# Two-pass stacked products of 64 rows and a split pooled product in a two-block network

## The chip, the cores and the metric

The kernel runs on one core of a Trainium2 chip. Its time is the device time of one execution in microseconds (us), given as the median of several runs. The core has a matrix engine (PE), a vector engine (DVE), an activation engine (ACT), a general engine (POOL), a sync engine (SP) that mostly issues DMAs, and DMA engines that move data. Each engine works through its own list of instructions in order.

## The reference, cut to what matters

The program takes 512 tokens of width 1024 through two blocks. The first block has an "even" mixer (multi-scale pooling beside a state-space scan) and an "odd" mixer (gated convolution). The second block has four feed-forward layers and two mixers: `mix0` (differential attention beside an RWKV-7 layer) and `mix1` (native sparse attention, "NSA", beside an mLSTM). All in float32. What the change touches:

```python
# even mixer: four groups of 128 channels
mixed = einsum('bsgc,gcd->bsgd', pooled, pool_w) * pool_scale
# mix0, differential attention: 4 heads, 2 components of 64 each
s = einsum('bhcqd,bhckd->bhcqk', q, k);  p = softmax(where(mask, s, -1e30))
attn = p[:, :, 0] - lam_full * p[:, :, 1]
# mix0, RWKV-7: low-rank gates of rank 64, 64 and 128
w = -softplus(-(w0 + tanh(wl) @ w2)) - 0.5;  a = sigmoid(a0 + al @ a2);  g = sigmoid(gl) @ g2
# mix1, NSA: 8 heads of 64 in 2 groups, three sets of keys
sc = einsum('bghqd,bgnd->bghqn', q, k_cmp)   # 31 compressed blocks
ss = q @ ks;  sw = q @ kw                    # selected (all 8 blocks here) and window keys
```

## The kernel before, in words

Activations lie with channels on the 128 partitions and the 512 tokens along the free side. A "dense" product (`form1`) takes one 128-column slab of weights: SP loads it as float32 (tile `st`, 3 buffers), ACT writes its fp16 high part and DVE the fp16 remainder (`wh`, `wl`), and PE makes, for each 128 rows, three fp16 products (L309 to L311) into one PSUM bank. `split` (L290, L291) divides an activation in the same way: ACT writes the high part, POOL (or DVE) subtracts to get the low part.

The order of the instructions on each engine is made by a scheduler when the program is built. It takes the program's order as priority, and raises the RWKV work of `mix0` over the rest. PSUM banks and SBUF tiles come from pools with fixed buffer counts. A tile that shares a `tag` with another uses the same buffer, so it waits until the other one has been read.

`even` (the trace's 0 to 250 us): the pooled groups multiply `pool_w` by the pooled tile `pd` in one float32 product each (L818).

`mix0` (about 850 to 1212 us): 22 dense products are made in `AB_ORDER`. After the v of each RWKV head pair, `rwkv_prepare` runs for that pair; `rwkv_solve` and `rwkv_chain` follow. `rwkv_prepare` loads `lora` (tile of its own), makes two float32 products of 64 rows by 512 columns (L1022, L1050) with the shared tile `wa`, and later inverts 16 by 16 blocks from the tile `Lb` (L1096, L1098). `rwkv_chain` makes one float32 product of 128 rows with the gate tile `gs` (L1234). Each of four differential heads gets q and k through `rope` (four DMAs that swap halves, L994; two POOL products, L995 and L996; one DVE sum, L997), then for each of four query tiles two float32 score products of 64 rows (L1268), softmax, and the values. At the end `project_out` adds the result to x: first the heads 0 to 2, then the rest, which needs the last head and the last RWKV pair.

`mix1` (about 1910 to 2210 us): the queries of one pair of heads at a time are made, rotated and split into `nq`. `nsa_pair` then makes, for each query tile and each of three key sets, six fp16 products of 64 rows (L1573): high-high, low-high, high-low, each for the two heads of the pair, which lie on rows 0 to 63 and 64 to 127. The keys stand in two copies with the halves exchanged (`ks`, `ksx`). The rope of the next pair's query shares the buffers of the tag `swap` with `nw`, which the pair before still uses.

A float32 product appears as two instructions in the trace.

Of the kernel before, what the change touches and what calls it, by code (L numbers as in the profile page):

```python
# [10 lines left out]
F32 = mybir.dt.float32  # L11
# [14 lines left out]
FS = 16.0  # L26
NEG = -1e30
WINDOWS = (2, 4, 8, 16)
LAM_INIT = 0.8 - 0.6 * math.exp(0.0)
# [156 lines left out]
class Net:  # L186
# [106 lines left out]
    def later(self):  # L293

        if self.due:
            self.due[0] -= 1
            if not self.due[0]:
                _, v, r = self.due
                self.due = None
                self.reciprocal(v, r)  # L300

    def form1(self, src, kn, xh, xl, w=None):
# [462 lines left out]
    def even(self):  # L765
        nc, A = self.nc, self.A
        V, G = nc.vector, nc.gpsimd
        with ExitStack() as c:
# [5 lines left out]
            tp = open_("e_t")  # L774
            pw = self.const(sp, "pool_w", [P, 4, P])
            cnt = self.const(sp, "c_cnt", [P, 4, 16])
            vec = self.const(sp, "ev_vec", [P, 2, 4])
# [18 lines left out]
            yl = self.parts("hl")  # L796

            for g in range(4):
                ps = self.form1(A["ev_in"][4 + g], KD, hh, hl)
# [207 lines left out]
    def rwkv_prepare(self, i, K, sp, tk, wk, r, k, v):  # L1007
# [16 lines left out]
        nc.scalar.activation(ld, ps, AF.Tanh, scale=0.5, bias=K["w0h"][:, i:i + 1])  # L1024
        cd = -0.5 * math.exp(-0.5)
# [22 lines left out]

        ps = self.aux()
        nc.tensor.matmul(ps, lora[64:128], K["wa"][64:128], start=True, stop=True)  # L1050
        a = tt("ta")
        nc.scalar.activation(a, ps, AF.Tanh, scale=0.5, bias=K["a0h"][:, i:i + 1])
        V.tensor_scalar(a, a, 0.5, 0.5, op0=ALU.mult, op1=ALU.add)
# [150 lines left out]
    def rwkv_chain(self, R, K, wk, yh, yl):  # L1204
# [5 lines left out]
        g2 = wk.tile([P, P], F32, name="g2")  # L1210
        nc.scalar.dma_start(g2, self.A["lora"][:, 1, i * P:(i + 1) * P])

        ps = self.aux().rearrange("p (a b) -> p a b", a=8)
# [39 lines left out]
    def diff_head(self, h, K, dk, yh, yl, q, k, vt):  # L1253
# [53 lines left out]
    def mix0(self):  # L1307
        nc, A = self.nc, self.A
        V, G = nc.vector, nc.gpsimd
        with ExitStack() as c:  # L1310
# [41 lines left out]
            V.scalar_tensor_tensor(K["lamf"], le[:, 0:1], LAM_INIT, le[:, 1:2], op0=ALU.add, op1=ALU.subtract)  # L1352
            K["wa"] = sp.tile([P, T], F32, name="wa")
            K["gs"] = sp.tile([P, T], F32, name="gs")
            yh = self.parts("hh")
# [28 lines left out]
            def take(n, ps):  # L1384
                if n < 2:
                    t = tk.tile([P, T], F32, name="ta")
                    shifted(ps, n, t)
                    if n == 0:
                        nc.scalar.activation(K["wa"][0:64], t[0:64], AF.Tanh)
                        V.tensor_copy(K["wa"][64:128], t[64:128])  # L1390
                    else:
                        nc.scalar.activation(K["gs"], t, AF.Tanh, scale=0.5)
                        V.tensor_scalar(K["gs"], K["gs"], 0.5, 0.5, op0=ALU.mult, op1=ALU.add)
                elif n < 14:
# [7 lines left out]
                else:  # L1402
                    h, j = divmod(n - 14, 2)
                    s = tk.tile([P, 1 + T], F32, name="raw", bufs=2)[:, :T]
                    self.scaled(s, ps)
                    d = dk.tile([P, T], F32, name="qr" if j == 0 else "kr", bufs=2)
                    self.rope(dk, d, s, cs)
                    got["qk"[j]] = d
                    if j == 1:
# [133 lines left out]

    def halves(self, pool, name, src, bufs=1, eng=None):

        r = pool.tile([P, 2, T], F16, name=name, bufs=bufs)
        self.split(r[:, 0], r[:, 1], src, eng)
        return r

    def nsa_pair(self, i, K, nk, yh, yl, q):  # L1550
# [6 lines left out]
        st = {}  # L1557
        hs = (slice(0, 64), slice(64, 128))

        def scores(qt, j):  # L1560
            n = (qt + 1) * P
            if j == 0:
                st[qt] = (nk.tile([P, 2, 3], F32, name="nmx", bufs=3), nk.tile([P, 2, 3], F32, name="nls", bufs=3))
                m, mask = 31, K["cmpm"][:, qt]
                keys = lambda hb, c: K["kcmp"][hs[hb], c, g * 31:g * 31 + 31]
            else:
                m, mask = n, K["causal"][:, 384 - qt * P:512]
                keys = lambda hb, c: K[("ks", "kw")[j - 1]][g != hb][hs[hb], c, :n]
# [109 lines left out]
    def mix1(self):  # L1678
        nc, A = self.nc, self.A
        V, G = nc.vector, nc.gpsimd  # L1680
        with ExitStack() as c:
# [34 lines left out]
            def keys(j):  # L1716
# [3 lines left out]
                self.rope(nk, s, s, cs)  # L1720
                d = self.halves(sp, n, s)
                e = sp.tile([P, 2, T], F16, name=n + "x")
                nc.sync.dma_start(e[0:64], d[64:128])
                nc.scalar.dma_start(e[64:128], d[0:64])
                K[n] = (d, e)

# [104 lines left out]
```

## Time and profile before

| | us |
|---|---|
| median of 3 runs (lowest, highest) | 2565.97 (2560.58, 2567.92) |
| profiled execution, its own time | 2559.88 |
| profiled execution, span from first to last instruction | 2558.1 |
| PE busy | 2462.0 (96%) |
| DVE busy | 1397.3 (55%) |
| ACT busy | 940.7 (37%) |
| POOL busy | 734.6 (29%) |

Busy time is the union of an engine's instructions. PE instructions overlap: a matmul's row tells how long one takes from entering to leaving, while the next may start earlier, so what a product costs is read from one start to the next. "Idle before, releaser" names what an engine's wait ended with.

### The profile page before, as it was taken

Reading aid. Unit: us, or ns where it says so; the run is one execution under the profiler, and the core shown is the slowest. Engines: PE = TensorE matmul, PEld = TensorE weight load, DVE = VectorE, ACT = ScalarE, POOL = GpSimd, SP = SyncE. Lnnn points to the kernel's source line nnn. Section 1 sums busy time; section 2 is a strip of 40 time slices with the busy share of each in tenths; the row PEclk is TensorE's granted clock in tenths of the full one; section 3 lists DMA queues with packets and bytes.
Section 4 is the critical chain, followed back from the end, with each engine's and each line's share of the span. In section 5 each row is a group of like instructions: output and inputs, shape, how many; then the busy total and the mean of one; then the engine's idle time right before and its main releaser. Section 6 shows DMA issues by size and latency. Waiting matters only on the chain.

```text
span 2558.1 us, 36794 instructions
## 1 busy us (share of the span) xinstructions
PE 2462.0 (96%) x14453; PEld 1259.9 (49%) x14453; DVE 1397.3 (55%) x2383; ACT 940.7 (37%) x1598; POOL 734.6 (29%) x657
## 2 busy tenths in 40 slices
PE   6998989999999999999999999999999999899998
PEld 3554434444444456674444444444457565444445
DVE  8945897743333767757433334333345777733334
ACT  3223665533322333334323223322232566523322
POOL 4820760333310332322333201333003122333300
PEclk9889999999999999999999999999999999999999
DMA  5314221233333321114333333333335201333334
GB/s 158 88 52 124 83 66 50 85 100 104 99 112 123 108 66 48 45 27 138 100 105 101 97 101 107 100 100 102 99 105 160 65 24 47 95 102 105 97 105 124
DMA packets 108853, 237.66 MB, mean 93 GB/s; under 512 B 38920, under 2 KB 48264, under 8 KB 108680
## 3 DMA queue, kind: packets, MB, share of 16 engines
q1 hardware_dynamic: 93024, 226.93, 29.5%
q10 hardware_dynamic: 15656, 8.39, 1.2%
q8 instruction: 113, 1.85, 0.3%
q14 instruction: 60, 0.49, 0.1%
HBM read 222.69 MB, written 7.34 MB: 90 GB/s over the span
## 4 chain that ended last, share of the span: by engine, by line
PE 82%; DVE 7%; issue 4%; POOL 4%; DMA 2%; ACT 1%; SPq 0%; POOLq 0%; ACTq 0%; DVEq 0%
PE b L310 16%; PE b L309 16%; PE b L311 16%; PE b L513 6%; PE b L512 6%; PE b L511 6%; POOL cv L928 3%; PE b L1155 1%; DVE wl L283 1%; PE b L1573 1%; PE mm L311 1%; PE mm L310 1%; PE b L1593 1%; PE mm L309 1%; PE b L1268 1%
## 5 line engine op out<-in xcount | busy, mean ns | idle before, releaser
L309 PE MATMUL b<-hh,wh 128*128 128x512 f16 x2096 | 795.4, 382 | 22.2 <-ACT hh L290 8.2
L282 ACT ACTIVATE wh<-st 128x1024 f16<-128x1024 f32 (+6 forms) x432 | 422.1, 979 | 1065.1 <-PE b L310 634.0
L310 PE MATMUL b<-hl,wh 128*128 128x512 f16 x2096 | 798.0, 381 | 1.0 <-POOL hl L291 1.0
L311 PE MATMUL b<-hh,wl 128*128 128x512 f16 x2096 | 796.6, 381 | 0.4 <-DVE wl L283 0.4
L283 DVE SCALAR_TENSOR_TENSOR wl<-st,wh 128x1024 f16<-128x1024 f32 (+6 forms) x432 | 512.7, 1188 | 331.1 <-ACT wh L282 330.3
L310 PEld LDWEIGHTS <-wh 128*128 128x128 f16 x2320 | 228.9, 99 | 292.5 <-issue 34.0
L309 PEld LDWEIGHTS <-wh 128*128 128x128 f16 x2320 | 229.4, 99 | 288.4 <-issue 19.7
L311 PEld LDWEIGHTS <-wl 128*128 128x128 f16 x2320 | 228.6, 99 | 284.1 <-issue 19.1
L513 PE MATMUL b<-fh,wl 128*128 128x512 f16 x660 | 250.4, 379 | 0.0
L512 PE MATMUL b<-fl,wh 128*128 128x512 f16 x660 | 250.4, 379 | 0.0
L511 PE MATMUL b<-fh,wh 128*128 128x512 f16 x660 | 250.3, 379 | 0.0
L500 POOL TENSOR_TENSOR sg<-sg,rho 128x512 f32<-128x512 f32 x88 | 153.5, 1746 | 292.8 <-ACT sg L499 282.2
L291 POOL TENSOR_TENSOR fl<-f,fh 128x512 f16<-128x512 f32 x88 | 139.7, 1587 | 265.7 <-ACT fh L290 265.5
L503 DVE SCALAR_TENSOR_TENSOR f<-b,sg 128x512 f32<-128x512 f32 x88 | 60.8, 691 | 246.1 <-PE b L311 240.0
L335 DVE TENSOR_TENSOR sg<-b,rho 128x512 f32<-128x512 f32 x88 | 60.4, 691 | 232.3 <-PE b L311 228.8
L291 POOL TENSOR_TENSOR hl<-nh,hh 128x512 f16<-128x512 f32 x45 | 59.5, 1329 | 298.4 <-ACT hh L290 298.4
L513 PEld LDWEIGHTS <-wl 128*128 128x128 f16 x660 | 64.6, 98 | 77.9
L512 PEld LDWEIGHTS <-wh 128*128 128x128 f16 x660 | 64.6, 98 | 77.9
L511 PEld LDWEIGHTS <-wh 128*128 128x128 f16 x660 | 64.6, 98 | 77.8
L309 PE MATMUL mm<-hh,wh 128*128 128x512 f16 x224 | 87.2, 393 | 10.6 <-ACT hh L290 8.7
L928 POOL TENSOR_TENSOR cv<-cv,cvt 128x512 f32<-128x512 f32 x60 | 88.1, 1470 | 15.2 <-ACT cvt L927 10.8
L310 PE MATMUL mm<-hl,wh 128*128 128x512 f16 x224 | 87.8, 394 | 3.2 <-POOL hl L291 2.0
(605 smaller groups left out, 3032.6 us busy)
## 6 DMA issues: line engine op xcount, KB each, us to landing
st<-in_gu_a SPq DMA_DIRECT2D x88, 512.0 KB, 3.5
st<-in_gu_b SPq DMA_DIRECT2D x88, 512.0 KB, 3.5
st<-in_dn_b SPq DMA_DIRECT2D x36, 512.0 KB, 3.5
st<-in_dn_a SPq DMA_DIRECT2D x32, 512.0 KB, 3.5
st<-in_od_in SPq DMA_DIRECT2D x24, 512.0 KB, 3.5
st<-in_ab_in SPq DMA_DIRECT2D x22, 512.0 KB, 3.6
st<-in_cd_in SPq DMA_DIRECT2D x16, 512.0 KB, 3.7
st<-in_ev_in SPq DMA_DIRECT2D x15, 512.0 KB, 3.7
```

The source lines that it names most:

```text
L282: nc.scalar.activation(wh[:, s], st[:, s], AF.Copy, scale=WS)
L283: nc.vector.scalar_tensor_tensor(wl[:, s], st[:, s], WS, wh[:, s], op0=ALU.mult, op1=ALU.subtract)
L291: (eng or self.nc.gpsimd).tensor_sub(lo, src, hi)
L309: self.nc.tensor.matmul(ps, wh[:, s], xh[:, k], start=(k == 0), stop=False)
L310: self.nc.tensor.matmul(ps, wh[:, s], xl[:, k], start=False, stop=False)
L311: self.nc.tensor.matmul(ps, wl[:, s], xh[:, k], start=False, stop=(k == kn - 1))
L500: nc.gpsimd.tensor_mul(sg, sg, self.rho)
L503: nc.vector.scalar_tensor_tensor(f, ps, 1.0 / FS, sg, op0=ALU.mult, op1=ALU.mult)
L511: nc.tensor.matmul(ps, wh[:, s], fh[:, k], start=(k == 0), stop=False)
L512: nc.tensor.matmul(ps, wh[:, s], fl[:, k], start=False, stop=False)
L513: nc.tensor.matmul(ps, wl[:, s], fh[:, k], start=False, stop=(k == KF - 1))
L928: G.tensor_add(cv, cv, t)
```

## The change

New helpers: `halves` (moved) splits a tile into high and low fp16 parts. `stack` copies these, by four DMAs within SBUF, so that for each 64-row half e the high part lies on its own rows and the low part on the other 64 rows of a 128-row tile. `twice` copies the high part of a 64-row half onto both halves, also by four DMAs. `stacked` makes scores from them: one product of 128 rows per head (high and low query parts against the high key parts, in one pass), and one of 64 rows (high query part against low key parts).

Differential scores, NSA scores and the two RWKV low-rank products of 64 rows use this form; the gate product and the pooled product become three fp16 products. The low-rank weights are loaded twice over (four DMAs a pair) into a tile that shares the tag `Lb`. `rope` of the differential heads now writes in place, and the stacked parts share the tag `swap`; in NSA the parts share the tag `sm`. The softmax tile `pe1` has one buffer instead of two.

```diff
+    def stack(self, dst, src):
+        for e, q in enumerate(HALF):
+            self.nc.sync.dma_start(dst[q, e], src[q, 0])
+            self.nc.sync.dma_start(dst[HALF[1 - e], e], src[q, 1])
+    def twice(self, dst, src):
+        for e, q in enumerate(HALF):
+            for h in HALF:
+                self.nc.sync.dma_start(dst[h, e], src[q])
+    def stacked(self, ps, l, r, rl):
+        for e in range(2):
+            self.nc.tensor.matmul(ps[e], l[:, e], r(e), start=True, stop=False)
+        for e, q in enumerate(HALF):
+            self.nc.tensor.matmul(ps[e], l[q, e], rl(e)[q], start=False, stop=True)
...
-                nc.tensor.matmul(pp, pw[:, g], d, start=True, stop=True)
+                dp = self.halves(ek, "pdp", d)
+                for a, b in ((0, 0), (0, 1), (1, 0)):
+                    nc.tensor.matmul(pp, pwp[:, a, g], dp[:, b], start=(a + b == 0), stop=(a == 1))
...
-        lora = wk.tile([P, P], F32, name="lora")
-        nc.scalar.dma_start(lora, self.A["lora"][:, 0, cols])
-        ps = self.aux()
-        nc.tensor.matmul(ps, lora[0:64], K["wa"][0:64], start=True, stop=True)
+        lora = wk.tile([P, 2, P], F32, name="lora", tag="Lb")
+        for j, q in enumerate(HALF):
+            for h in HALF:
+                nc.scalar.dma_start(lora[h, j], self.A["lora"][q, 0, cols])
+        nc.scalar.activation(lh, lora, AF.Copy, scale=WS)
+        V.scalar_tensor_tensor(ll, lora, WS, lh, op0=ALU.mult, op1=ALU.subtract)
+        def low_rank(j):
+            ps = self.aux()
+            nc.tensor.matmul(ps, lh[:, j], K["was"][:, j], start=True, stop=False)
+            nc.tensor.matmul(ps, ll[HALF[j], j], K["was"][HALF[j], j], start=False, stop=True)
+            return ps
...
-        nc.tensor.matmul(ps, g2, K["gs"], start=True, stop=True)
-        V.tensor_mul(y, y, ps)
+        for a, c in ((0, 0), (0, 1), (1, 0)):
+            nc.tensor.matmul(ps, gp[:, a], K["gs"][:, c], start=(a + c == 0), stop=(a == 1))
+        V.scalar_tensor_tensor(y, ps, IWS, y, op0=ALU.mult, op1=ALU.mult)
...
+            ps = [self.aux()[:, :n] for _ in range(2)]
+            self.stacked(ps, q[:, :, qt * P:(qt + 1) * P], lambda cp: k[0][:, cp, :n], lambda cp: k[1][:, :n])
             for cp in range(2):
-                b = slice(cp * 64, cp * 64 + 64)
-                ps = self.aux()[:, :n]
-                nc.tensor.matmul(ps, q[b, qt * P:(qt + 1) * P], k[b, :n], start=True, stop=True)
-                pe.append(self.soft(dk, ps, mask, n, mx[:, cp:cp + 1], ls[:, cp:cp + 1], f"pe{cp}", 2))
+                pe.append(self.soft(dk, ps[cp], mask, n, mx[:, cp:cp + 1], ls[:, cp:cp + 1], f"pe{cp}", 2 - cp))
...
-                        nc.scalar.activation(K["wa"][0:64], t[0:64], AF.Tanh)
-                        V.tensor_copy(K["wa"][64:128], t[64:128])
+                        nc.scalar.activation(t[0:64], t[0:64], AF.Tanh)
+                        self.stack(K["was"], self.halves(dk, "qp", t, tag="swap"))
...
-                    self.rope(dk, d, s, cs)
-                    got["qk"[j]] = d
+                    self.rope(dk, s, s, cs)
+                    if j == 0:
+                        self.stack(e, self.halves(dk, "qp", s, tag="swap"))
+                    else:
+                        self.split(kh, kl, s)
+                        self.twice(e, kh)
...
-            for a, c in ((0, 0), (1, 0), (0, 1)):
-                for hb in range(2):
-                    nc.tensor.matmul(ps[hb][:, :m], q[hs[hb], a, qt * P:(qt + 1) * P], keys(hb, c),
-                                     start=(a + c == 0), stop=(c == 1))
+            self.stacked([t[:, :m] for t in ps], q[:, :, qt * P:(qt + 1) * P], lambda _: keys(0), lambda _: keys(1))
...
-                qs[i] = self.halves(nk, "nq", s, 2)
+                qs[i] = nk.tile([P, 2, T], F16, name="nq")
+                self.stack(qs[i], self.halves(nk, "qp", s, 2, tag="sm"))
```

## Rows read from the trace of the kernel before

**Rows 1.** The page: busy time by engine, and the chain's shares.

```profile
PE 2462.0 (96%) x14453; PEld 1259.9 (49%) x14453; DVE 1397.3 (55%) x2383; ACT 940.7 (37%) x1598; POOL 734.6 (29%) x657
PE 82%; DVE 7%; issue 4%; POOL 4%; DMA 2%; ACT 1%; SPq 0%; POOLq 0%; ACTq 0%; DVEq 0%
```

**Rows 2.** Stretches: length, then busy (count) of PE, PEld, DVE, ACT, POOL; clock; DMA.

```profile
100.00:165.00 65.00, 59.76 (x345) 35.82 (x343) 47.20 (x85) 12.67 (x20) 35.18 (x57) 0.84 0.23 62
...
860.00:930.00 70.00, 61.26 (x465) 39.12 (x464) 52.42 (x102) 22.07 (x37) 29.23 (x26) 0.95 0.28 79
930.00:1080.00 150.00, 149.57 (x1633) 96.10 (x1634) 109.51 (x263) 51.95 (x106) 46.48 (x46) 1.00 0.19 49
1080.00:1110.00 30.00, 27.50 (x270) 19.55 (x266) 22.87 (x75) 9.47 (x25) 6.07 (x5) 0.89 0.10 21
1110.00:1190.00 80.00, 76.12 (x845) 49.73 (x845) 45.81 (x122) 28.58 (x72) 17.52 (x14) 1.00 0.26 74
2050.00:2190.00 140.00, 130.10 (x1227) 80.96 (x1226) 105.09 (x324) 89.11 (x280) 32.75 (x44) 0.98 0.11 31
```

**Rows 3.** PE's groups by line: busy us, mean ns of one, idle before.

```profile
L1268 PE MATMUL b<-kr,qr 64*128 64x128 f32 (+3 forms) x64 | 23.6, 482 | 0.0
...
L818 PE MATMUL a<-pd,pool_w 128*128 128x512 f32 x8 | 7.2, 997 | 3.7 <-DVE pd L812 3.7
...
L1022 PE MATMUL b<-wa,lora 64*128 64x512 f32 x8 | 4.5, 641 | 0.0
...
L1234 PE MATMUL b<-gs,g 128*128 128x512 f32 x8 | 4.1, 600 | 0.0
```

**Rows 4.** PE's timeline (start, us, what) around one low-rank product.

```profile
913.09 0.38 PE L310 MATMUL b<-hl,wh 128*128 128x512 f16 x1
913.40 1.12 PE L1022 MATMUL b<-wa,lora 64*128 64x512 f32 x2
914.45 0.39 PE L311 MATMUL b<-hh,wl 128*128 128x512 f16 x1
```

**Rows 5.** PE's timeline: passes of one NSA unit of 512 keys.

```profile
2031.07 0.39 PE L1573 MATMUL b<-ks,nq 64*128 64x512 f16 x1
2031.07 0.39 PE L1573 MATMUL b<-ksx,nq 64*128 64x512 f16 x1
2031.30 0.38 PE L1573 MATMUL b<-ks,nq 64*128 64x512 f16 x1
...
2031.51 0.38 PE L1573 MATMUL b<-ks,nq 64*128 64x512 f16 x1
```

**Rows 6.** L1573 alone: PE busy in the stretch of NSA, and the compressed keys' share.

```profile
1960.00:2190.00 230.00, 31.45 (x288) 12.00 (x288) 0.99 0.16 48
L1573 PE MATMUL b<-kcmp,nq 64*128 64x31 f16 x96 | 5.8, 178 | 0.0
```

**Rows 7.** The split of a query: duration ns min/median/max.

```profile
L290 ACT ACTIVATE nq<-sm x4: 615/629/630, 1952.0 to 2150.8; 128x512 f16<-128x512 f32 x4
L291 POOL TENSOR_TENSOR nq<-sm,nq x4: 1153/1155/1160, 1952.7 to 2151.5; 128x512 f16<-128x512 f32 x4
```

**Rows 8.** Rope's DMAs within SBUF: issue time on SP, and landing.

```profile
L994 SPq DMA_DIRECT2D swap<-raw x32: 507/586/1887, 872.7 to 1136.9; - x32
...
DMA to landing us min/median/max: 1.9/2.0/3.8
```

**Rows 9.** Timelines of POOL and PE where the second query becomes ready.

```profile
2061.27 1.15 POOL L291 TENSOR_TENSOR nq<-sm,nq 128x512 f16<-128x512 f32 x1 [2.48 <-ACT nq L290]
...
2063.03 0.19 PE L1573 MATMUL b<-kcmp,nq 64*128 64x31 f16 x2
```

**Rows 10.** DVE's timeline: the last read of the first pair's Lb.

```profile
921.97 0.16 DVE L1096 TENSOR_TENSOR xtmp<-Lb,Xb 64x15 f32<-64x15 f32 x1
```

**Rows 11.** POOL and DVE: the last head's and the last pair's results.

```profile
1178.64 1.16 POOL L291 TENSOR_TENSOR hl<-do,hh 128x512 f16<-128x512 f32 x1 [2.12 <-ACT hh L290]
...
1188.13 0.69 DVE L291 TENSOR_TENSOR hl<-y,hh 128x512 f16<-128x512 f32 x1 [0.69 <-ACT hh L290]
```

More of the change, by code (lines that the diff above doesn't have):

```diff
@@ L27 @@
 NEG = -1e30
+HALF = (slice(0, 64), slice(64, 128))
 WINDOWS = (2, 4, 8, 16)
@@ L300, in later, with halves @@
                 self.reciprocal(v, r)
+    def halves(self, pool, name, src, bufs=1, eng=None, tag=None):
+        r = pool.tile([P, 2, T], F16, name=name, bufs=bufs, tag=tag or name)
+        self.split(r[:, 0], r[:, 1], src, eng)
+        return r
+    def stack(self, dst, src):
[11 more added lines that the diff above has]
+            self.nc.tensor.matmul(ps[e], l[q, e], rl(e)[q], start=False, stop=True)
     def form1(self, src, kn, xh, xl, w=None):
@@ L775, in even @@
             pw = self.const(sp, "pool_w", [P, 4, P])
+            pwp = sp.tile([P, 2, 4, P], F16, name="pwp")
             cnt = self.const(sp, "c_cnt", [P, 4, 16])
@@ L796, in even @@
             yl = self.parts("hl")
+            nc.scalar.activation(pwp[:, 0], pw, AF.Copy, scale=WS)
+            V.scalar_tensor_tensor(pwp[:, 1], pw, WS, pwp[:, 0], op0=ALU.mult, op1=ALU.subtract)
+            V.tensor_scalar(vec[:, 0], vec[:, 0], IWS, None, op0=ALU.mult)
             for g in range(4):
@@ L1017, in rwkv_prepare @@
         pairs = lambda t: t.rearrange("p (a e b) -> p a e b", a=4, e=2)
-        lora = wk.tile([P, P], F32, name="lora")
-        nc.scalar.dma_start(lora, self.A["lora"][:, 0, cols])
-        ps = self.aux()
-        nc.tensor.matmul(ps, lora[0:64], K["wa"][0:64], start=True, stop=True)
+        lora = wk.tile([P, 2, P], F32, name="lora", tag="Lb")
+        for j, q in enumerate(HALF):
+            for h in HALF:
+                nc.scalar.dma_start(lora[h, j], self.A["lora"][q, 0, cols])
+        lh = wk.tile([P, 2, P], F16, name="lh")
+        ll = wk.tile([P, 2, P], F16, name="ll")
+        nc.scalar.activation(lh, lora, AF.Copy, scale=WS)
[5 more added lines that the diff above has]
+            return ps
+        ps = low_rank(0)
         ld = tt("ta")
-        nc.scalar.activation(ld, ps, AF.Tanh, scale=0.5, bias=K["w0h"][:, i:i + 1])
+        nc.scalar.activation(ld, ps, AF.Tanh, scale=0.5 * IWS, bias=K["w0h"][:, i:i + 1])
         cd = -0.5 * math.exp(-0.5)
@@ L1047, in rwkv_prepare @@
         G.tensor_mul(KR[:, 1], r, pt)
-        ps = self.aux()
-        nc.tensor.matmul(ps, lora[64:128], K["wa"][64:128], start=True, stop=True)
+        ps = low_rank(1)
         a = tt("ta")
-        nc.scalar.activation(a, ps, AF.Tanh, scale=0.5, bias=K["a0h"][:, i:i + 1])
+        nc.scalar.activation(a, ps, AF.Tanh, scale=0.5 * IWS, bias=K["a0h"][:, i:i + 1])
         V.tensor_scalar(a, a, 0.5, 0.5, op0=ALU.mult, op1=ALU.add)
@@ L1211, in rwkv_chain @@
         nc.scalar.dma_start(g2, self.A["lora"][:, 1, i * P:(i + 1) * P])
+        gp = wk.tile([P, 2, P], F16, name="gp")
+        nc.scalar.activation(gp[:, 0], g2, AF.Copy, scale=WS)
+        V.scalar_tensor_tensor(gp[:, 1], g2, WS, gp[:, 0], op0=ALU.mult, op1=ALU.subtract)
         ps = self.aux().rearrange("p (a b) -> p a b", a=8)
@@ L1352, in mix0 @@
             V.scalar_tensor_tensor(K["lamf"], le[:, 0:1], LAM_INIT, le[:, 1:2], op0=ALU.add, op1=ALU.subtract)
-            K["wa"] = sp.tile([P, T], F32, name="wa")
-            K["gs"] = sp.tile([P, T], F32, name="gs")
+            K["was"] = sp.tile([P, 2, T], F16, name="was")
             yh = self.parts("hh")
@@ L1388, in take @@
                     if n == 0:
-                        nc.scalar.activation(K["wa"][0:64], t[0:64], AF.Tanh)
-                        V.tensor_copy(K["wa"][64:128], t[64:128])
-                    else:
-                        nc.scalar.activation(K["gs"], t, AF.Tanh, scale=0.5)
-                        V.tensor_scalar(K["gs"], K["gs"], 0.5, 0.5, op0=ALU.mult, op1=ALU.add)
+                        nc.scalar.activation(t[0:64], t[0:64], AF.Tanh)
+                        self.stack(K["was"], self.halves(dk, "qp", t, tag="swap"))
+                    else:
+                        nc.scalar.activation(t, t, AF.Tanh, scale=0.5)
+                        V.tensor_scalar(t, t, 0.5, 0.5, op0=ALU.mult, op1=ALU.add)
+                        K["gs"] = self.halves(sp, "gs", t)
                 elif n < 14:
@@ L1405, in take @@
                     self.scaled(s, ps)
-                    d = dk.tile([P, T], F32, name="qr" if j == 0 else "kr", bufs=2)
-                    self.rope(dk, d, s, cs)
-                    got["qk"[j]] = d
+                    self.rope(dk, s, s, cs)
+                    e = dk.tile([P, 2, T], F16, name="qr" if j == 0 else "kr", bufs=2)
+                    if j == 0:
+                        self.stack(e, self.halves(dk, "qp", s, tag="swap"))
+                        got["q"] = e
+                    else:
+                        kh = dk.tile([P, 2, T], F16, name="kh", tag="swap")[:, 0]
+                        kl = dk.tile([P, T], F16, name="kl", bufs=2)
+                        self.split(kh, kl, s)
+                        self.twice(e, kh)
+                        got["k"] = (e, kl)
                     if j == 1:
@@ L1542, in compress @@
         return r
[L1544 to L1548, printed above, removed]
     def nsa_pair(self, i, K, nk, yh, yl, q):
@@ L1557, in nsa_pair @@
         st = {}
-        hs = (slice(0, 64), slice(64, 128))
         def scores(qt, j):
@@ L1564, in scores @@
                 m, mask = 31, K["cmpm"][:, qt]
[L1565 removed]
+                keys = lambda c: K["kcmp"][:, c, g * 31:g * 31 + 31]
             else:
                 m, mask = n, K["causal"][:, 384 - qt * P:512]
[L1568 removed]
+                keys = lambda c: K[("ks", "kw")[j - 1]][:, g, c, :n]
             mx, ls = st[qt]
             ps = [self.aux(), self.aux()]
[L1571 to L1574 removed]
+            self.stacked([t[:, :m] for t in ps], q[:, :, qt * P:(qt + 1) * P], lambda _: keys(0), lambda _: keys(1))
             st[qt, j] = [self.soft(nk, ps[hb][:, :m], mask, m, mx[:, hb, j:j + 1], ls[:, hb, j:j + 1], "npe",
@@ L1720, in keys @@
                 self.rope(nk, s, s, cs)
[L1721 to L1725, printed above, removed]
+                K[n] = sp.tile([P, 2, 2, T], F16, name=n)
+                self.twice(K[n], self.halves(nk, "kp", s, 2, tag="sm"))
             nv = K["nv"] = sp.tile([P, 2, 4, 256], F16, name="nv")
```

## The prediction

> **What bounds the kernel now.** I read the page's busy times and chain first. PE is busy for 96% of the span and 82% of the chain that ended last is PE's, so time is made or lost on PE [rows 1]. An average over stages doesn't say whether the stages that are changed have that limit, so I cut the span into stretches next. In the middle of `mix0` PE is busy 149.57 of 150 us. At its start, where the first RWKV pair has to be prepared, it is idle 8.7 of 70 us; between 1080 and 1110 us 2.5 of 30; in the last 80 us 3.9. In the NSA part of `mix1` 9.9 of 140 us are idle, and in the even mixer's stretch 5.2 of 65, at a granted clock of 0.84 of full [rows 2]. The reader is to see two kinds of stage: one in which a product taken off PE is time gained, and one (both ends of `mix0`, NSA) in which PE is nearly full, but with filler: dense products that run while a chain of softmax, rope and DMA steps goes on. Then I read the removed products by line, and their spacing in the timeline, since a row's duration is longer than the time it keeps PE [rows 3 to 6].
>
> **The change part by part: products.** A dense fp16 product of 512 columns keeps PE for 0.22 us: passes start at 2031.07, 2031.30 and 2031.51 [rows 5]. A float32 product of 64 rows keeps it for 1.05 us, from 913.40 to 914.45 [rows 4].
>
> Differential scores: they occupy 23.6 us now [rows 3]. After, each of 16 units (4 heads, 4 query tiles) takes two passes of 128 rows and two of 64. The two of 64 rows read different rows and write different banks. In NSA two such products start at the same 2031.07 [rows 5], so I count them as one pass: three passes a unit. From below: an NSA unit, which has three such passes now, costs (31.45 - 5.8) / 32 = 0.80 us, waits and tails included [rows 6], so 16 units cost 12.8 and 10.8 us are freed. From above: by spacing alone, 0.216 us at 512 columns and in proportion for 384, 256 and 128, a unit is 3 x 0.135 = 0.41 us, 16 are 6.5, and 17.1 are freed. I take 13, nearer to the measured unit.
>
> When PE goes from 128-row to 64-row products, 0.31 us pass instead of 0.22 (913.09 to 913.40) [rows 4]: about 0.095 us a switch. The Trainium skill, "TensorEngine Tiling (Array Packing)", section "Tiling Modes", says that changing the tiling mode, not just the tile, drains the engine. That speaks against mixing both heights in one unit; the row agrees. By that rule each unit pays two switches, 16 x 2 x 0.095 = 3.0 us, and 14.1 would be freed; without it, 17.1.
>
> Low rank: eight products, one row stands for both lines [rows 3]. Now 8 x 1.05 = 8.4 us; after, two passes of 0.216, plus up to two switches: 0.43 to 0.62 us. That frees 3.4 to 5.0; I take 4. Gate product: 4.1 us for four [rows 3]; after, 4 x 3 x 0.216 = 2.6. That frees 0.9 to 1.5; I take 1.
>
> NSA scores: three passes side by side become two full ones and one side by side, three again [rows 5]. Nothing is freed, though the words "two passes" suggest a third. Bounds: 2 us gained through fewer instructions (192 for 288), 4.6 lost if each of 48 units gets one switch more. I take 0.
>
> Pooled product: 7.2 us for four [rows 3] become 12 passes of 0.22 to 0.43 us (full or half clock), 2.6 to 5.2. It frees 2 to 4.6 on PE. But this stage isn't PE's alone [rows 2], and the product now waits for a split of 0.63 + 1.15 us [rows 7] behind `pd`; the weights' one split stands early. I take 0 for the stage, bounds -4 and +6 us.
>
> **What is added on waits.** One split is 0.63 us on ACT and 1.15 on POOL [rows 7]. Four DMAs within SBUF take SP 4 x 0.586 = 2.3 us to issue, the last lands 2.0 later [rows 8]. From the end of the split that is 4.3 us. With `rope`'s own four issues seen as short as 4 x 0.507, it is 4.0.
>
> Mix0: q, k and the low-rank input each get split and copies: 0.63 + 1.15 + 4.3 = 6.1 us later. In the 150 us in which PE is full the dense products cover that. POOL gets ten splits, 12 us, and has over half its time free there; SP gets 36 more issues, 21 us of 350, and weight loads queue behind them: three buffers are the cover. The cover is thin at two ends. First, the low-rank input comes before the first pair, where PE already idles. Second, the last head ends at 1179.8, and the last pair at 1188.8, before the rest of `project_out` can run [rows 11]: a head 6 us later eats most of 9 us of slack. `pe1` with one buffer adds a wait behind DVE's combination in each tile. The low-rank load shares `Lb`: the first pair's inversion reads it until 922.1 [rows 10], so the second pair's first product, at 913.40 now [rows 4], can't start before 922.1 + 2.3 (issue) + 2.0 + 0.6 (conversion, about a split of half the size) = 927, 13 us later. What is queued behind it is that pair's own work; PE has dense products instead. From below these delays cost 0, from above 18 (13 for the pair, 5 at the ends); I take 4, since only about 12 of these 350 us are idle now.
>
> Mix1: queries 2 to 4 are made only when the pair before lets go of the shared buffer. At the second, POOL's split ends at 2062.42 and the scores start at 2063.03, 0.6 us later; the others look the same [rows 9]. So each of the three waits gets 4.3 us of copies. All three on the path: 12.9 us. None: 0, as dense products fill PE while they last. PE is 93% busy there [rows 2], so most of a delay is filled at once, but filler used early is missing at the end. I take 4.
>
> **Sum.** -(13 + 4 + 1) + 4 + 4 + 0 = -10 us. The profiled execution took 2559.88 us (span 2558.1, 1.8 around it), so 2550 in its terms. It lies 6.1 below the median of the runs shown, 2565.97. So the forecast for the median is 2556, its own range 2547 to 2563.
>
> **The rivals.** First, the freed time comes back as waiting: the ends of `mix0` and the four NSA pairs are chains of ACT, DVE, POOL and DMA, and PE's dense products only fill them. For it: 2.5 of 30 us idle at 1080, and scores that start 0.6 us after their query. Against it: 150 us with 0.4 idle, where nothing but PE can be the limit. Then of the 18 us freed only those of the two middle heads and pairs, 9, shorten the stage, and the copies give them back, 4.3 at its start and 5 at the last head; with 4 in NSA that is +4, 2570.
>
> Second, on the other side: the second pair's wait for `Lb` goes through the whole RWKV chain. For it: `mix0`'s last 25 us can't start before the last pair's result [rows 11], the pairs follow one another through shared tiles, and the wait is certain in its place. Against it: PE is full at 930 to 1080, so a pair that comes later finds other work done first. If the chain decides, the stage moves by +13, less the 5 that its own products save, and the other savings turn idle; with +4 in NSA, 2566 + 8 + 4 = 2578. It decides from the point at which the second pair has less than 13 us of slack against the dense products.
>
> Third, all 18 are kept and no delay shows: 2548.
>
> Fourth, the change doesn't do what it says: the two halves do not run side by side, being fed after a pass of full height. Then 48 units get a fourth pass, 16 in `mix0` (16 x 0.135 = 2.2) and 32 in NSA (4.3): 2556 + 6.5 = 2562.5.
>
> **How the numbers follow.** Forecast 0.42; freed time back as waiting 0.25; the `Lb` wait 0.15; all kept 0.13; no side by side 0.05. What this kernel's runs can tell from no change is about 0.3%, 7.7 us: faster is below 2558.3, slower above 2573.7. The forecast's range lies on the faster side for 0.85 of its chance, the rest within. Faster: 0.36 + 0.13 + 0.02 from the first rival = 0.51. Slower: 0.15 + 0.03 = 0.18. Within: 0.31. The range 2540 to 2576 goes from all kept with the upper bound of the scores (2548, less 4 for 17.1 instead of 13, and the even mixer's 4) to just below the full `Lb` case, and leaves about 0.2 outside.
>
> **What would show it.** Right: the score group of the differential heads at 7 to 13 us instead of 23.6; half products of 64 rows starting in pairs; the NSA group's 31.45 within 2 us; low-rank products 0.43 to 0.62 us from start to next start; `mix0` shorter by 12 to 16 us; NSA's scores starting about 5 us after the split. Wrong: PE's idle time in `mix0` up by over 12 us, or the second pair's first low-rank product behind the first pair's inversion with idle PE after it; NSA's stretch longer by over 9; or a difference in the feed-forward layers, which the change does not touch.

## The result and the profile after

The changed kernel takes 2596.74 us (median of 4 runs, 2594.1 to 2597.83) against 2566.94 before (4 runs): ratio 1.0119 [1.0099, 1.0138], 30 us slower. The forecast was 2556 (2540 to 2576), faster. Its profiled execution took 2594.1 us, 34 more than that of before.

The page after, busy times and chain, hardly differs from [rows 1]: PE 95% busy, 81% of the chain.

```profile
PE 2470.4 (95%) x14365; PEld 1267.1 (49%) x14365; DVE 1399.0 (54%) x2392; ACT 951.1 (37%) x1621; POOL 752.6 (29%) x671
PE 81%; DVE 7%; POOL 4%; issue 4%; DMA 2%; ACT 2%; SPq 0%; ACTq 0%; POOLq 0%; DVEq 0%
```

By stage it does. `mix0` and `mix1` whole, before (first two rows) and after, columns as in [rows 2]:

```profile
836.00:1213.00 377.00, 361.22 (x3428) 226.35 (x3427) 263.90 (x607) 134.77 (x273) 112.36 (x104) 0.98 0.25 71
1900.00:2207.00 307.00, 291.11 (x2387) 178.99 (x2385) 217.65 (x544) 161.50 (x430) 72.53 (x84) 0.98 0.25 76
```
```profile
845.00:1223.00 378.00, 355.02 (x3438) 223.81 (x3437) 264.80 (x613) 142.52 (x291) 122.53 (x115) 0.97 0.28 78
1909.00:2241.00 332.00, 299.51 (x2286) 186.37 (x2285) 213.48 (x542) 162.46 (x430) 73.64 (x84) 0.94 0.25 74
```

A stage's length is PE's idle time, plus what is lost to a lower granted clock (length times one less the clock), plus the rest, PE's work at full clock (the clock is rounded, which is up to 2 us a stage). `mix0`: 15.8 + 7.5 + 353.7 before, 23.0 + 11.3 + 343.7 after. PE has 10 us less work, and not one is left in the length. `mix1`: 15.9 + 6.1 + 285.0 before, 32.5 + 19.9 + 279.6 after: 5 us less work, 31 more of waiting and lower clock, 25 us longer. The feed-forward layers stay; the even mixer, at 253 us, is 7 longer. That these 7 us are the pooled product's isn't shown: in the profiles of the experiments that leave the even mixer alone, `mix0` starts anywhere from 836 to 846 us (836 before, 845 after).

The stretches after that answer to [rows 2] (the stages start 9 us later): the 150 us in which PE idled 0.4 now hold 5.6 idle, the last 80 us of `mix0` 10.3 instead of 3.9, NSA's 140 us 17.8 instead of 9.9.

```profile
939.00:1089.00 150.00, 144.43 (x1677) 97.32 (x1675) 112.14 (x270) 56.68 (x122) 55.00 (x53) 1.00 0.23 58
1119.00:1199.00 80.00, 69.66 (x707) 44.75 (x704) 44.04 (x122) 25.03 (x65) 13.55 (x11) 0.87 0.19 60
2059.00:2199.00 140.00, 122.24 (x1004) 76.60 (x1003) 94.76 (x291) 80.52 (x257) 34.44 (x40) 0.91 0.13 36
```

PE's groups after, answering to [rows 3]: pooled product, differential full and half passes, gate, the two low-rank passes.

```profile
L851 PE MATMUL a<-pdp,pwp 128*128 128x512 f16 x12 | 5.1, 524 | 5.2 <-ACT pdp L291 5.2
...
L325 PE MATMUL b<-kr,qr 128*128 128x128 f16 (+3 forms) x32 | 10.0, 317 | 0.0
L327 PE MATMUL b<-kl,qr 64*128 64x128 f16 (+3 forms) x32 | 9.4, 317 | 0.0
L1282 PE MATMUL b<-gs,gp 128*128 128x512 f16 x12 | 3.3, 381 | 0.8 <-DVE y L1278 0.8
L1062 PE MATMUL b<-was,lh 128*128 128x512 f16 x8 | 2.5, 380 | 0.0
L1063 PE MATMUL b<-was,ll 64*128 64x512 f16 x8 | 1.9, 386 | 0.0
```

The NSA scores (full, then half passes) take 24.14 + 22.46 us of PE where one group took 31.45 [rows 6]: the two halves of a unit seldom stand next to each other in PE's list (of 64 such pairs, counting both attentions, 15 start within 20 ns of each other; of the 144 pairs of NSA passes before it were 87).

```profile
1980.00:2215.00 235.00, 24.14 (x96) 0.95 0.18 52
1980.00:2215.00 235.00, 22.46 (x96) 0.95 0.18 52
```

A lone half also pays for the change of height on both sides. Between 512-column products of 128 rows, starts are 0.216 us apart; from 128 to 64 rows and back it is 0.32 each way, as [rows 4] had it for one case:

```profile
956.31 0.39 PE L325 MATMUL b<-kr,qr 128*128 128x512 f16 x1
956.63 0.39 PE L327 MATMUL b<-kl,qr 64*128 64x512 f16 x1
956.95 0.39 PE L337 MATMUL b<-hl,wh 128*128 128x512 f16 x1
957.17 0.38 PE L338 MATMUL b<-hh,wl 128*128 128x512 f16 x1
```

The way of the fourth query before, and after, the timeline that answers to [rows 9]:

```profile
2150.79 0.63 ACT L290 ACTIVATE nq<-sm 128x512 f16<-128x512 f32 x1 [3.22 <-DVE sm L997]
2152.65 0.19 PE L1573 MATMUL b<-kcmp,nq 64*128 64x31 f16 x2
```

```profile
2164.86 2.45 SPq L1027 DMA_DIRECT2D swap<-sm  x4
...
2170.85 0.34 PE L1668 MATMUL b<-ident,no 128*128 128x128 f32 x1 [2.11 <-POOL no L1658]
...
2173.99 0.63 ACT L291 ACTIVATE qp<-sm 128x512 f16<-128x512 f32 x1 [1.02 <-DVE sm L1030]
2174.65 1.14 SPq L312 DMA_DIRECT2D nq<-qp  x2
...
2175.99 1.10 SPq L313 DMA_DIRECT2D nq<-qp  x2
2176.65 1.09 PE L1718 MATMUL b<-ident,num 128*128 128x128 f32 x4 [5.46 <-DVE num L1715]
...
2178.06 0.19 PE L325 MATMUL b<-kcmp,nq 128*128 128x31 f16 x1 [0.32 <-DMA nq<-qp]
```

From ACT's part of the split (2173.99) to the first score it is 4.1 us; before it was 1.9 here. At the second and third query it is 7.4 and 7.3 for 2.4. While the fourth is rotated and split, PE waits 2.1 and 5.5 us for other chains, the longer one at the end of an mLSTM head's, where the load of the same transposes waited 0.3 before:

```profile
PEld b L1673 <- DVE num L1670: 0.3, 1, 0.3
```

For the copies themselves PE then waits 0.3 us (last row after). That it finds nothing else to do because filler was used up earlier is my reading; no run shows it directly.

### The profile page after: what moved, and what is told of

The parts are those of the page before. It is cut to its first block, busy times and chain, and to the rows that moved or that the text cites. A ratio compares the mean times of both kernels' runs of the same rounds, so it can differ in the third digit from the quotient of the medians.

```text
span 2592.3 us, 36817 instructions
## 1 busy us (share of the span) xinstructions
PE 2470.4 (95%) x14365; PEld 1267.1 (49%) x14365; DVE 1399.0 (54%) x2392; ACT 951.1 (37%) x1621; POOL 752.6 (29%) x671
## 4 chain that ended last, share of the span: by engine, by line
PE 81%; DVE 7%; POOL 4%; issue 4%; DMA 2%; ACT 2%; SPq 0%; ACTq 0%; POOLq 0%; DVEq 0%
PE b L336 16%; PE b L337 16%; PE b L338 16%; PE b L539 5%; PE b L540 5%; PE b L538 5%; POOL cv L961 3%; PE b L1638 1%; PE mm L336 1%; PE mm L337 1%; PE mm L338 1%; PE b L327 1%; PE b L1199 1%; DVE wl L284 1%; PE b L1648 1%
## 5 line engine op out<-in xcount | busy, mean ns | idle before, releaser
L284 DVE SCALAR_TENSOR_TENSOR wl<-st,wh 128x1024 f16<-128x1024 f32 (+6 forms) x432 | 506.5, 1173 | 337.7 <-ACT wh L283 336.5
L961 POOL TENSOR_TENSOR cv<-cv,cvt 128x512 f32<-128x512 f32 x60 | 89.0, 1486 | 15.2 <-ACT cvt L960 10.8
```

Source lines behind the costliest of these rows:

```text
L284: nc.vector.scalar_tensor_tensor(wl[:, s], st[:, s], WS, wh[:, s], op0=ALU.mult, op1=ALU.subtract)
L961: G.tensor_add(cv, cv, t)
```

## The experiments

Medians in us; in brackets that of the kernel before in the same comparison. mix0 and mix1: length, idle time, granted clock of the profiled execution (before: 377, 15.8, 0.98 and 307, 15.9, 0.98). A profile is one execution: e3's lies 19 us above its median, e2's 8 above, e12's 6 below. In the kernels that leave a stage alone, `mix0` takes 375 to 387 us and `mix1` 304 to 310, so a difference of 25 us in `mix1` is safe and one of 5 or 10 in `mix0` is not.

| | median | ratio, 95% interval | mix0 | mix1 |
|---|---|---|---|---|
| e1 pooled | 2575.71 (2563.94) | 1.0040 [1.0025, 1.0055] | 387, 16.1, 0.96 | 304, 17.3, 0.99 |
| e2 differential | 2575.88 (2563.94) | 1.0040 [1.0022, 1.0058] | 390, 20.2, 0.93 | 310, 17.4, 0.97 |
| e3 low rank, gate | 2567.20 (2563.94) | 1.0011 [0.9999, 1.0024] | 392, 19.2, 0.94 | 308, 17.1, 0.97 |
| e4 NSA | 2590.02 (2563.94) | 1.0102 [1.0086, 1.0119] | 377, 15.7, 0.98 | 334, 33.1, 0.93 |
| e5 NSA, no copies | 2581.71 (2564.36) | 1.0059 [1.0034, 1.0083] | 380, 13.9, 0.97 | 323, 22.2, 0.94 |
| e6 NSA, copies only | 2583.82 (2564.36) | 1.0086 [1.0067, 1.0105] | 375, 14.3, 0.99 | 328, 29.7, 0.94 |
| e7 NSA, own buffers | 2586.78 (2564.36) | 1.0090 [1.0068, 1.0112] | 376, 15.5, 0.98 | 328, 27.9, 0.94 |
| e8 NSA, paired | 2592.69 (2564.36) | 1.0121 [1.0102, 1.0139] | 377, 12.3, 0.97 | 336, 37.3, 0.92 |
| e9 all but NSA | 2569.08 (2564.32) | 1.0015 [1.0004, 1.0025] | 381, 24.1, 0.96 | 305, 15.2, 0.98 |
| e10 three half passes | 2578.60 (2564.32) | 1.0057 [1.0039, 1.0076] | 393, 25.0, 0.94 | 307, 16.6, 0.98 |
| e11 differential, no copies | 2552.27 (2564.32) | 0.9951 [0.9936, 0.9965] | 372, 20.2, 0.98 | 306, 14.6, 0.98 |
| e12 NSA, full passes twice | 2602.26 (2564.32) | 1.0139 [1.0117, 1.0162] | 379, 14.5, 0.97 | 341, 32.4, 0.93 |
| e13 differential, engines | 2557.20 (2562.49) | 0.9982 [0.9972, 0.9993] | 372, 15.8, 0.98 | 308, 16.8, 0.98 |
| e14 NSA with filler | 2601.14 (2562.49) | 1.0148 [1.0131, 1.0165] | 383, 15.1, 0.96 | 342, 28.8, 0.94 |
| e15 before with filler | 2563.91 (2562.49) | 1.0005 [0.9993, 1.0018] | 376, 12.2, 0.97 | 308, 8.7, 0.98 |
| e16 e13, low rank too | 2564.71 (2562.51) | 1.0007 [0.9994, 1.0019] | 380, 22.4, 0.96 | 309, 17.6, 0.98 |
| e17 NSA, engines | 2576.41 (2562.51) | 1.0049 [1.0031, 1.0067] | 380, 13.8, 0.97 | 320, 22.5, 0.96 |
| e18 pooled, high part | 2566.79 (2562.51) | 1.0013 [1.0003, 1.0024] | 378, 14.2, 0.98 | 309, 18.5, 0.97 |

Theory: what is put behind the split (copies, shared buffers) delays chains that PE can no longer fill. Rivals: the passes themselves (B); the granted clock, which falls when PE idles (C). Outside every range that was expected came e2 (9 us above), e11 (8 below) and, by 3 us or less, e3, e6, e7, e8, e10, e16 and e17.

**Each part alone** (e1 to e4: the hunks of one part on the kernel before) and **all but NSA** (e9).

> The kernel before with the pooled product alone changed. If the parts act in their own stages (theory A), the even mixer ends 7 us later (253 instead of 246 us), because the product waits for a split of 0.63 us on ACT and 1.15 us on POOL, and the time is about 2574, with the other stages as before within 2 us. If the stages' lengths come from a new order of the whole program (rival B), the even mixer is within 2 us of before and the time within 5 us of 2567.

> The kernel before with the differential scores alone changed. Theory A: PE's work on these scores falls from 23.6 to some 15 us (four passes, seldom side by side), and mix0 (377 us before) gets 3 to 8 us shorter, so 2559 to 2564; the low-rank part then costs what this gains. Rival B: mix0 stays within 2 us, since its chain of pairs ends it: 2567.

> The kernel before with the low-rank and gate products alone changed. Theory A: the load that shares the buffer of Lb holds the second pair up by some 13 us, and mix0 gets 3 to 8 us longer though PE has 5 us less to do: 2570 to 2575. Rival B: dense products fill the wait, and mix0 is 3 to 5 us shorter: 2562 to 2564.

> The kernel before with the NSA scores, keys and queries alone changed. Theory A: mix1 takes 332 us instead of 307, as in the whole change: 2590 to 2594. Rival B: the 25 us come in part from what runs before mix1 (prefetched loads, buffers), and the part alone costs under 15 us: below 2582.

> The whole change except its NSA part. By the prediction's terms without NSA: -13 - 4 - 1 + 4 = -14 us, 2550 to 2553. If the savings of mix0 turn into waiting and lower clock, as the parts by themselves showed (+10, +11 and +1): 2568 to 2585. If NSA alone is the loss and the rest is worth nothing: 2560 to 2568. mix0 then at 363 (first), 377 to 390 (second), 377 (third).

No part gains (e3 can't be told from 0). NSA alone costs 26 us, and the change without it 5, so NSA is most of the 30. The parts sum to 53: they aren't additive. Stages that a part doesn't touch move too (e1: `mix0` 387 at a clock of 0.96 instead of 377 at 0.98), so a single profile can't price an edit of a few us.

**Differential scores: copies or passes?** e11 feeds the passes from the split, leaving out the placing of the parts; e13 lets the engines write the parts to their places; e10 has three fp16 half products, nothing stacked. All three also take the parts out of the shared buffers of `swap`, so DMAs and sharing aren't told apart: "copies" means both.

```diff
 e11
-   self.stack(e, self.halves(dk, "qp", s, tag="swap"))   # and twice(e, kh)
+   e = self.halves(dk, "qr" if j == 0 else "kr", s, 2)
 e13
+   for u, b in enumerate(HALF):
+       nc.scalar.activation(e[b, u], s[b], AF.Copy)      # k: also e[HALF[1 - u], u]
+       G.tensor_sub(e[HALF[1 - u], u], s[b], e[b, u])    # k: kl[b]
 e10
+   for a, c in ((0, 0), (1, 0), (0, 1)):
+       for cp, b in enumerate(HALF):
+           nc.tensor.matmul(ps[cp], q[b, a, qt * P:(qt + 1) * P], k[b, c, :n], ...)
```

> The kernel before, with the differential scores as three fp16 products of 64 rows for each half, the two halves in turn so that they can run side by side, straight from the split: no stacking and no copies (output correct). If copies and unpaired passes ate the saving: 10 to 17 us of PE time are kept, 2548 to 2556, mix0 363 to 370. If PE's time in mix0 isn't the limit, or freeing it only lowers the granted clock: 2562 to 2576, mix0 at 375 to 390, idle time and half clock up by what PE lost in work.

> The differential scores as in the changed kernel, in two stacked passes and two halves, but fed straight from the split without copies (the scores are other numbers, the instructions are the same). Against the differential part alone (2576 when it ran): if the copies delay heads, 8 to 15 us back, 2560 to 2567; if the delay is the passes or the clock, 2572 to 2580.

> The differential part alone with the stacked products of the change, but the engines write the parts to their places (ACT: two copies of 64 rows for q and four for k; POOL: the low parts, two of 64 rows, written to the other half), no DMA (output correct). If the DMAs behind the split cost the stage its gain: close to the kernel without copies (2552 when it ran), 2552 to 2560, that is 4 to 12 us under the kernel before. If what the extra work on ACT and POOL (4 x 0.6 and 2 x 1.2 us a head) delays is as bad: 2564 to 2576. The granted clock of mix0 decides between the two ends: 0.98 in the first case, 0.93 to 0.95 in the second.

`mix0` of e2, e11, e13 and e10, in this order:

```profile
844.00:1234.00 390.00, 369.77 (x3431) 233.48 (x3430) 266.70 (x608) 140.51 (x282) 122.46 (x113) 0.93 0.27 74
```
```profile
836.00:1208.00 372.00, 351.79 (x3433) 220.42 (x3432) 261.39 (x608) 141.34 (x283) 124.55 (x113) 0.98 0.26 73
```
```profile
843.00:1215.00 372.00, 356.20 (x3430) 223.06 (x3429) 265.45 (x606) 150.58 (x298) 130.26 (x120) 0.98 0.25 72
```
```profile
843.00:1236.00 393.00, 367.95 (x3464) 231.13 (x3463) 265.81 (x606) 141.06 (x283) 119.95 (x112) 0.94 0.24 68
```

The passes without copies gain 12 us, and the DMA copies turn that into a loss of 12. Work at full clock is nearly the same in e2 and e11 (342.5 and 344.4, from 353.7); so is idle time, 20.2. What differs in these profiles is the clock, 27 against 7 us lost, and over all runs too: a mean clock of 0.971 in e2's ten and of 0.980 in e11's four is 23 us of the span. Half of the 20 us lies in one place. e2 waits 1.4 us for RWKV's `W` at 1040 us and then runs 20 us at half clock; e11 waits 1.3 us at 1034 and stays at full clock (first the waits, then the stretches behind them, e2 and e11):

```profile
PE b L1214 <- DVE W L1205: 1.4, 1, 1.4
PE b L1270 <- ACT nsq L1255: 1.3, 1, 1.3
```
```profile
1043.00:1063.00 20.00, 20.00 (x154) 15.52 (x152) 7.85 (x31) 5.06 (x14) 5.36 (x5) 0.50 0.11 19
1034.00:1054.00 20.00, 19.11 (x269) 15.51 (x270) 9.72 (x20) 9.38 (x18) 7.63 (x6) 1.00 0.13 33
```

Neither wait is for a copy, so how the copies lower the clock isn't shown. Written by the engines, 5 us remain, at the clock of the kernel before (0.977 against 0.978): e13 is faster than both kernels. e10 went the other way than I thought: the same 344 us of work, no copies, and 14 us slower, with 5 more idle and 24 lost to the clock. Why is open.

**NSA: copies or passes?** e5 has the passes without copies, leaving out the placing of the parts; e6 has the copies of the queries (with the shared buffers of `sm`) without the passes, e17 parts written by ACT and POOL; e7 gives the first parts a buffer of their own; e8 holds a unit in the order full, full, half, half.

```diff
 e5
+   qs[i] = self.halves(nk, "nq", s, 2)                   # keys: K[n] = self.halves(sp, n, s)
 e6 (products as before)
+   qp = self.halves(nk, "qp", s, 2, tag="sm")
+   for h in HALF:
+       for a in range(2):
+           nc.sync.dma_start(qs[i][h, a], qp[h, a])
 e7
-   self.halves(nk, "kp", s, 2, tag="sm")                 # and the first "qp"
+   self.halves(ms, "kp", s, 1, tag="nms")
 e8 (order only, no waiting)
+   for n, p in zip(o[1:], o):
+       self.tc.add_manual_dep(n.ins, p.ins.name, NoSync)
 e17
+   nc.scalar.activation(qs[i][b, u], s[b], AF.Copy)
+   G.tensor_sub(qs[i][HALF[1 - u], u], s[b], qs[i][b, u])   # keys likewise, both halves
```

> The NSA part alone, with the stacked products but without the copies: the halves of the split are fed straight to the passes (the parts are not stacked, so the scores are other numbers; the instructions and their shapes are the same). Theory A (the copies and the shared buffers ahead of the queries make the loss): within 4 us of the kernel before, mix1 at 305 to 311 us against 306.5. Theory B (the passes themselves: halves that no longer run side by side, PE busy 46.6 us instead of 31.5): most of the +26 us stays, 2580 to 2590, mix1 322 to 333. Theory C (a lower granted clock because PE is idler): between them, and the clock of the stage falls with the idle time.

> The kernel before with its own NSA products, but each query's two parts go through four DMAs to their place before the products read them, as in the changed kernel. Theory A: 4 queries x 4.3 us and the shared buffer, +10 to +18 us, 2574 to 2582, PE idle in mix1 up by 8 to 16 us. Theory B: within 5 us of before. Theory C: as A, with the granted clock of mix1 below 0.96 where PE idles.

> The NSA part of the change alone (2590 us when it ran), but the parts of the two keys and of the first query are split into a buffer of their own and no longer take turns in the two buffers of the projections. If the shared buffers cause the first query's 13 us of delay: 8 to 13 us back, 2577 to 2582. If that delay is only the copies' own time or the passes: 0 to 3 us back, 2587 to 2590.

> The NSA part of the change alone (2590 us when it ran), with the four passes of a unit held in the order full, full, half, half, so that the two halves can start together. Theory B: the halves start side by side in most units and 32 x 0.22 to 0.44 us = 7 to 14 us come back, 2576 to 2583. Theory A: halves pair, PE's score time falls from 46.6 to some 32 us, but the stage stays as long, 2586 to 2592, since what the order frees is filled with waiting, or is lost because the first pass now has to wait for two score banks.

> The NSA part alone (2590 us when it ran), its parts written in place by ACT and POOL instead of by DMAs (output correct). If the DMAs are the loss: 2562 to 2570. If the passes lose as much by themselves as in the kernel without copies (2582): 2578 to 2586. If the extra work on ACT and POOL is as late as the DMAs: 2586 to 2592.

The copies alone cost 19 us and the passes alone 17, both together 26. Without DMAs 14 remain (e17). So theory A and rival B are both right, and overlap. They lose the time in different places. The four pairs' first scores come 69, 163, 207 and 253 us into the stage before, 71, 165, 210 and 267 in e6, 72, 163, 208 and 254 in e5: of e6's 21 us more, 14 lie ahead of the last pair, of e5's 16 nearly all behind its first score. The stretch from that score on, of before, e6 and e5:

```profile
2152.00:2179.00 27.00, 26.75 (x234) 14.12 (x232) 19.46 (x73) 16.24 (x58) 2.47 (x5) 1.00 0.12 37
```
```profile
2167.00:2201.00 34.00, 33.36 (x257) 16.66 (x255) 22.26 (x78) 18.27 (x61) 2.04 (x5) 0.97 0.16 46
```
```profile
2161.00:2203.00 42.00, 39.77 (x238) 19.60 (x238) 25.72 (x83) 20.47 (x65) 5.67 (x7) 0.81 0.11 32
```

In e5 PE waits for the fourth query's split (first row), and the pair goes at a clock of 0.81, which is 8 of its 15 us.

```profile
PE b L325 <- ACT nq L291: 3.5, 1, 3.5
PE b L1640 <- POOL no L1630: 2.1, 1, 2.1
```

In e8 the halves do pair, 47 of 48, and the score group (full, half) falls from 46.3 (e4) to 35.3 us of PE. The stage is no shorter, 336 for 334: 4 us more idle, and more lost to the clock. So with the copies in place the order of the halves gives nothing back; whether it would in e5, where nothing else is late, wasn't tried.

```profile
1975.00:2215.00 240.00, 21.93 (x96) 0.94 0.17 52
1975.00:2215.00 240.00, 13.41 (x96) 0.94 0.17 52
```

e7 starts the first pair 8 us earlier and gets about 4 of them.

**Is it the clock?** e12 issues each full NSA pass twice; e14 and e15 put unread products ahead of each mLSTM head's last transposes, 16 on e4 and 8 on the kernel before.

```diff
 e12
+   for last in (True, False):
+       self.nc.tensor.matmul(ps[e], l[:, e], r(e), start=True, stop=last)
 e14, e15
+   for _ in range(16):
+       nc.tensor.matmul(ps, k[:, 0, 0:P], q[:, 0], start=True, stop=True)
```

> The NSA part alone (2590 us when it ran), with each of the 64 full passes issued twice (the second overwrites the first, the output is the same): some 64 x 0.2 to 0.37 = 13 to 24 us more work for PE. If PE is the limit in the four pairs: 2600 to 2612. If the chains of the pairs and PE's idle time set the stage: 2586 to 2597, the work fills idle time, idle falls from 33 us to 20 to 25 and the granted clock of mix1 rises from 0.934.

> The NSA part alone (2590 us when it ran) with 16 products of 512 columns that nothing reads put on PE ahead of each of the four mLSTM heads' last transposes, where PE waited 5.5 us ahead of the fourth query and then ran at 0.6 to 0.7 of its clock for 20 us. If the loss of clock follows the idle time: the products cost 4 x 3.5 us of PE but fill that wait, the granted clock of mix1 rises from 0.934 to 0.96 or more, and the time stays or falls, 2578 to 2591. If PE's work is what counts: 2598 to 2606.

> The kernel before with 8 such products ahead of each of the four heads' last transposes. PE waits little there (0.3 us by the profile), so nothing is filled: +4 to +8 us, 2568 to 2572, if added PE work counts in full; within 3 us if the stage has that much slack.

Rival C fails in the form in which I put it: e14's clock in `mix1` stays at 0.94, and it is 12 us slower than e4. But the test is weak. The wait ahead of the fourth query falls from 5.5 to 2.9 us, and the half clock behind it from 14 to 7; other waits grow, and the stage's idle time falls by 4 us only, to 28.8. So what part of the loss is the clock's stays open. e12 too pays for its added work (+12). Work taken off PE here (e8) is not gained, and work added is paid for. In the kernel before it isn't: e15's 32 products, 6.9 us by spacing, go into idle time (15.9 to 8.7).

**Low rank and pooled product.** e16 adds the low-rank passes to e13, without DMAs for the parts; e18 drops the pooled input's low part.

```diff
 e16
+   nc.scalar.activation(lh[b, u], lora[b], AF.Copy, scale=WS)   # and lh[HALF[1 - u], u]
+   V.scalar_tensor_tensor(ll[b], lora[b], WS, lh[b, u], op0=ALU.mult, op1=ALU.subtract)
 e18
-   dp = self.halves(ek, "pdp", d)
+   nc.scalar.activation(dp, d, AF.Copy)
```

> e13's differential scores (2557 when it ran, 5 us under the kernel before), and the low-rank products as stacked passes too, their parts also written in place by ACT and DVE, with the weights in their own tile as before (output correct). By the prediction's term for them 3.4 to 5 us of PE are freed: 2552 to 2555. If the four conversions and their place ahead of each RWKV pair delay the pairs, or the work freed turns idle: 2557 to 2564.

> The pooled product alone, with the high part of its input only (left out: the low part, its split on POOL and one of three passes). The pooled part alone took 2576 when it ran, 11 over before. If the wait for POOL's split is that loss: 2560 to 2567. If it is the granted clock of the stages or the passes: 2570 to 2578.

The low rank's freed PE time isn't kept (e16 is 7.5 us above e13); idle time in `mix0` rises from 15.8 to 22.4, and its clock falls from 0.98 to 0.96. Of the pooled part's 12 us, 7.5 go with the low part, but not as the wait that I named: PE waits 5.2 us for ACT's `pdp` in both. In the profiles they go from the even mixer (254 to 248 us) and from `mix0` (387 to 378), which the part doesn't touch.

## Why the prediction was wrong

The forecast was 41 us too low, and none of the rivals comes near 2597; the highest was 2578. By stage the sum had -14 us for `mix0`, +4 for `mix1` and 0 for the even mixer; the profiled executions have +1, +25 and +7.

- **Work freed in `mix0`: nearly right.** PE's work there fell by 11 us with the differential scores alone (e2; 13 forecast) and by 4 with low rank and gate (e3; 5 forecast), but by 12 and not 18 with both (e9), the clock being rounded. The sign I had set for it failed all the same: the score group was to be busy for 7 to 13 us and is for 10.0 + 9.4, its halves standing alone. e11's 12 us are these 13 only in part: its `mix0` is 5 us shorter, with 9 less work and 4 more idle time, and some 8 of the 12 are a higher mean clock over all runs (0.980 against 0.977).
- **The step that failed first: "Mix1 ... I take 4" with "NSA scores ... I take 0".** The NSA part costs 26 us. The copies put 5, 5 and 2 us behind the splits of queries 2 to 4, 12 for 12.9 at most as worked out. But I took that sum for the upper end of their cost, and it isn't where the time went. After, the pairs' first scores come 8, 10, 9 and 16 us later in the stage than before, and the last pair takes 35 us instead of 27. So 8 of the 25 us are gone before the first score, for which the sum had no term (with a buffer of their own for the first parts, e7, the first pair is 8 us earlier); 1 goes at queries 2 and 3, so there the copies were hidden nearly as forecast; 7 go ahead of the fourth and 8 behind it. The copies alone (e6) cost 19. And passes equal in number weren't equal in time: 17 us (e5), against a bound of 4.6. What in the passes does that is open; the lost pairing was tried only with the copies in place, and gave nothing back there (e8).
- **The second: "From below these delays cost 0, from above 18 ... I take 4".** The copies of `mix0` cost 24 us (e2 against e11), outside the bound, and more than the scores free. In the profiles they cost it as granted clock, a term that the sum did not have, and not as idle time, by which I had sized the 4 (the rows add up to 15.5 us idle, not 12 [rows 2]). The copies aren't the only way to that loss: e10 has none, and 24 us are lost to the clock. The first rival (freed time comes back as waiting, 2570) names half of this: e9, the change without NSA, came to 2569 and not to 2552, and of 12 us less work in `mix0` 8 came back as idle time and 8 as lost clock.
- **The `Lb` wait** was where it was put: the second pair's weights are issued at 936.3, just behind the last read of the first pair's `Lb` (forecast 922.1, with the stage 9 later 931). The products were forecast for 927, so 936; they ran at 955 and 958, 32 us later in the stage than before and not 13 [rows 4].

```profile
936.14 0.15 DVE L1140 TENSOR_TENSOR xtmp<-Lb,Xb 64x15 f32<-64x15 f32 x1
936.33 0.49 ACTq L1054 DMA_DIRECT2D lora<-in_lora  x1
...
955.01 0.60 PE L1062 MATMUL b<-was,lh 128*128 128x512 f16 x2
958.13 0.39 PE L1063 MATMUL b<-was,ll 64*128 64x512 f16 x2
```

  It didn't decide the stage: the last pair ended 2 us later in it, the last head 5 earlier, than in [rows 11].

```profile
1182.79 1.16 POOL L292 TENSOR_TENSOR hl<-do,hh 128x512 f16<-128x512 f32 x1 [3.94 <-ACT hh L291]
...
1199.40 0.69 DVE L292 TENSOR_TENSOR hl<-y,hh 128x512 f16<-128x512 f32 x1 [0.70 <-ACT hh L291]
```

- **No side by side** (0.05, +6.5): true for most units; undone with the copies in place, it gives no time back (e8).
- **Pooled product**: 0 (-4 to +6) was too low; alone it is +12, in its profile mostly in a stage that it doesn't touch.

## What to carry over

In a stage where PE is full only because filler runs beside a chain, a saving on PE and a delay of the chain do not cancel: in `mix1` 5 us less work came with 17 more of idle time and 14 more lost to the clock. Price such an edit at the chain's first and last links, where the pairs' starts moved, and not by the stage's mean; and ask what the granted clock will do, since in `mix0` it took what the scores had freed. When data has to change its place among the partitions, let the engine that makes it write it there: here that made the difference between a loss of 12 us and a gain of 5 in `mix0` (e2, e13), and between 26 and 14 us of loss in `mix1` (e4, e17), with the shared buffers gone as well.

## What the hardware showed beyond this

The granted clock moves runs of one kernel by as much as the edits: e2's ten runs go from 2561.9 us at a mean clock of 0.977 to 2583.7 at 0.966. Half clock (1.2 instead of 2.4 GHz) came after a wait of 1.4 us in e2 and not after one of 1.3 in e11, and shortening a wait of 5.5 us did not bring the stage's clock back (e14). The Trainium skill, "TensorE: Matmul & The Clock Gate", section "What's actually happening", says that how many products run at the low level varies from run to run of one kernel. e2's runs agree, with 0.85% between their times. The same section puts the penalty of the ramp to full clock under 1% of a typical span. Here the clock falls again and again within a run, and e2's runs lose 2.3 to 3.4% of their span to it.

ACT and POOL can write 64 rows to the other 64 partitions while they convert (e13, e17): no DMA is needed for stacking. Converting 64 rows takes them as long as 128: 0.63 us on ACT and 1.15 to 1.19 on POOL in e13, against 0.63 and 1.15 [rows 7].
